# Seven block products instead of eight in three of eight units of the late gate and up pairs

## The chip, the cores and the metric

The kernel runs on one core of one Trainium2 chip. The metric is device time in microseconds. Three runs of the kernel before gave a median of 1877.37 us (1877.36 to 1877.59).

## The reference, cut to what matters

One layer of a decoder with 256 tokens of width 2048: a mixer (gated linear attention and sparse attention, merged), then a gated feed-forward block, then a norm. All is float32. The change touches the feed-forward block, whose weights are 2048 x 11264 (gate and up side by side) and 5632 x 2048:

```python
def swiglu(h, w_gate_up, w_down):
    g, u = jnp.split(h @ w_gate_up, 2, axis=-1)
    return (jax.nn.silu(g) * u) @ w_down
...
        h = rms_norm(x, norm2_gain[layer]) * (1.0 + sc2) + sh2
        x = x + g2 * swiglu(h, w_ffn_gate_up[layer], w_ffn_down[layer])
    return rms_norm(x, final_norm_gain)
```

## The kernel before, in words

**A block product.** TensorE takes a 128 x 128 block of activations as the stationary operand and streams 128 x 512 of weights past it. To keep float32 accuracy, both are split in two parts, a rounded one (float32r, "hi") and what is left (the rest, "lo"). One block product is three matmuls into one PSUM bank: hi by hi, hi by lo, lo by hi (L351 to L353 in `main`). The activations are split once (tiles `h`, `gA`, `gB`); the weights are split as they arrive: ScalarE casts (L311) and VectorE subtracts (L313), 1024 columns at a time.

**An item** (`Mm`) is four contraction blocks of 128 rows by 512 columns, 1 MB, loaded by one DMA from SP (L272) into one of three `raw` buffers. It has two token halves, so 4 x 2 x 3 = 24 matmuls. `hi` and `lo` have four buffers of 1024 columns each, two of which an item takes.

**The order** is written out: the list `items`, walked by `run`. After the matmuls of an item come (where it is the last of its group) the evacuation, the preparing of items ahead (`pres`, two ahead) and one step of each of the side threads (`qa`, `qb`, `qc`), as far as a credit of 3.6 us an item allows. Each engine works its own queue in the order in which this loop issues.

**The feed-forward block** has three parts of 4, 4 and 3 column blocks of 512 (`FF_PARTS`). In each part, each column block has a gate group and an up group (four items each, two of the four main PSUM banks each), then four down groups follow over the part's columns. The gate is evacuated by a Silu (L1240), the up by a product (L1244); the result is transposed on TensorE (L1057, eight transposes a block, in two steps of the thread `qb`, into the three auxiliary banks `pa`), cast (L1062) and its rest formed (L1063). The down groups read it; `need` waits for the transposes of the last block. A down group's evacuation adds to the residual (L1278, L1279).

**PSUM** has eight banks: four main (`pm`), three auxiliary (`pa`), one held (`ph`, used earlier in the attention).

**Row buffers.** `g2_start` (L1263) loads the gate's row and the final gain's row into the two `gr` buffers, on ScalarE's DMA queue. `acc` is one more buffer of 2048 columns.

Of the kernel before, what the change touches and what calls it, by code (L numbers as in the profile page):

```python
# [35 lines left out]
SLOT = 3.6  # L36
ORDER = "d0 a0 a1 d1 a2 a3 d2 y0 y1 d3 y2 y3"
FF_PARTS = ((0, 4), (4, 4), (8, 3))
NEG = -1.0e30
FILL = -3.0e38  # L40
TAKEN = -3.4e38
# [16 lines left out]
        self.ahead = AHEAD  # L58


class Grp:
    def __init__(self, act, evac, need=None, late=False, cost=0.6):
        self.act, self.evac, self.need, self.late, self.cost, self.ps = act, evac, need, late, cost, None
        self.mid = None


class Lr:
# [41 lines left out]
def tile_layer(tc, x, c, positions, norm1_gain, norm2_gain, w_ada, b_ada, w_in, gate_up, gate_bias,  # L109
# [3 lines left out]
    with (  # L113
# [140 lines left out]
        def load(it):  # L254
            if it.extra:
                raw = work("raw", EARLY_RAWS, [128, D])
            else:
                raw = stp.tile([128, D], F32, tag="raw", bufs=RAW_BUFS, name=name("raw"))
            if isinstance(it, Mm):
# [12 lines left out]
            sp.dma_start(it.raw, src)  # L272
# [15 lines left out]
        def pre_mm(it, rests_last=False):  # L288
# [28 lines left out]
            for rest in rests:  # L317
                yield
                rest()

        def pre(its):

            gens = [(pre_ada if isinstance(it, Ada) else pre_mm)(it) for it in its]
            while gens:
                for g in gens[:]:
                    if next(g, gens) is gens:
                        gens.remove(g)

        def main(it):
            if isinstance(it, Lr):  # L330
                ps = psum_main()
                for kt in range(KT):
                    pe.matmul(ps[0:32], it.both[:, kt].rearrange("p v n -> p (v n)"),
                              h1[:, kt].rearrange("p a t -> p (a t)"), start=kt == 0, stop=kt == KT - 1)
                it.evac(ps)
                return
            g = it.grp
            if it.first:
                g.ps = [psum_main() for _ in range(2)]
                g.deferred = []  # L340
            parts = [(hv[:, k], lv[:, k]) for hv, lv in it.hl for k in range(hv.shape[1])]

            def products(it, parts, k, t):
                kt = it.k0 + k
                if g.need:
                    g.need(kt, t)
                xh, xl = g.act(kt)
                hv, lv = parts[k]
                o = g.ps[t][:, 0:it.nc]
                a, b = xh[:, t * 128:(t + 1) * 128], xl[:, t * 128:(t + 1) * 128]  # L350
                pe.matmul(o, a, hv, start=it.first and k == 0, stop=False)  # L351
                pe.matmul(o, a, lv, start=False, stop=False)  # L352
                pe.matmul(o, b, hv, start=False, stop=it.last and k == it.nk - 1)  # L353

            for k in range(it.nk):
                for t in range(1 if it.defer or it.by_token else 2):
                    products(it, parts, k, t)
            if it.defer or it.by_token:
                g.deferred.append((it, parts))
            if it.by_token:  # L360
                for d, dparts in g.deferred:
                    for k in range(d.nk):
                        if g.mid and d is it and k == MID:
                            g.mid(g.ps)
                        products(d, dparts, k, 1)
            it.hl = None

        def run():
# [47 lines left out]
            for it in items:  # L416
# [10 lines left out]
                if late_evac:  # L427
                    late_evac()
                    late_evac = None
                early_evac = isinstance(it, Mm) and it.last and it.by_token  # L430
# [617 lines left out]
                qb.add(m_transposes(n))  # L1048
            return f

        def split_transposes(src, kt0, dst):

            for i in range(2):
                ps = psum_aux()
                for a in range(2):
                    for t in range(2):
                        pe.transpose(ps[:, a * S + t * 128:a * S + t * 128 + 128],  # L1057
                                     src[:, t, (i * 2 + a) * 128:(i * 2 + a + 1) * 128], ident)
                kt = kt0 + i * 2
                hi = dst[kt // 8][:, kt % 8:kt % 8 + 2, :].rearrange("p a t -> p (a t)")  # L1060
                lo = dst[2 + kt // 8][:, kt % 8:kt % 8 + 2, :].rearrange("p a t -> p (a t)")
                act.copy(hi, ps)  # L1062
                dve.tensor_sub(lo, ps, hi.bitcast(F32))  # L1063
                yield 0.7
# [180 lines left out]
                    qb.add(ff_transposes(a, kt0))  # L1245
            return f

        def ff_transposes(a, kt0):
# [4 lines left out]
            for cost in split_transposes(a, kt0, late["act"]):  # L1253
                late["ready"] += 2
                yield cost

# [5 lines left out]

        def g2_start():  # L1263
            late["g2"] = bcast_row("gr", b_ada[5 * D:6 * D])
            late["fg"] = g8("gr")
            act.dma_start(late["fg"], final_gain.unsqueeze(0).to_broadcast([128, D]))

        def g2_rows():
            for n in range(4):
# [46 lines left out]
        for p, (g0, ng) in enumerate(FF_PARTS):  # L1316
            ex = spread(0) if p == 0 else None
            at_first = len(items)
            for n in range(ng):
                if p == 0 and n == 1:  # L1320
                    items.append(Call(g2_start))
                for which in range(2):
                    add_group(w_ffn_up, which * DFF + (g0 + n) * 512, 512,
                              Grp(act_h2, up_evac(which, n, n * 4), need_h2), extra=ex if n else None)
# [57 lines left out]
```

## Time and profile before

| what | value |
|---|---|
| median of 3 runs | 1877.37 us |
| the profiled execution | 1878.03 us |
| its span (first to last instruction) | 1875.9 us |
| TensorE busy | 1832.3 us, 98% |
| VectorE busy | 1285.0 us, 69% |
| ScalarE busy | 853.4 us, 45% |
| GpSimd (POOL) busy | 115.4 us, 6% |
| granted TensorE clock, mean | 0.994 |

Busy shares are means over the whole span. In the span's second half the table of 40 slices has VectorE at 4 to 7 tenths and the DMA engines at 5 to 8, and TensorE at 9 in every slice but the last, which is 8. PE is TensorE, PEld its weight loads, DVE VectorE, ACT ScalarE; a name with q is the DMA issue of that engine. A matmul's shown duration includes its way through the array, so consecutive ones overlap; the pitch is read from the starts.

### The profile page before, as it was taken

How to read it: one execution, taken by the hardware profiler on the slowest of the kernel's cores; microseconds unless marked ns; L12 is line 12 of the kernel's file. 1: busy time of each engine (PE TensorE's matmuls, PEld its weight loads, DVE VectorE, ACT ScalarE, POOL GpSimd, SP SyncE). 2: the span in 40 equal slices, each digit the busy share in tenths (PEclk: the TensorE clock that was granted, in tenths of full speed). 3: DMA queues.
4: the chain of work that ended last, by engine and by line, in shares of the span. 5: the costliest groups of instructions: out<-in, count | busy, mean ns of one | idle time of the engine just before them, and what ended most of it. 6: DMA issues, size and time to landing. Idle time of an engine off the chain costs nothing.

```text
span 1875.9 us, 23110 instructions
## 1 busy us (share of the span) xinstructions
PE 1832.3 (98%) x9132; PEld 1507.8 (80%) x9132; DVE 1285.0 (69%) x1441; ACT 853.4 (45%) x1114; POOL 115.4 (6%) x141
## 2 busy tenths in 40 slices
PE   3999999999999999999999999999999999999998
PEld 2888888877788888888888787888788888888886
DVE  6899865798765678787778566777555445554455
ACT  4554443655645444444444445444334444334443
POOL 0000000533220100200000000000000000000002
PEclk8999999999999999999999999999999999999999
DMA  9998743534445787888888754889555555655553
GB/s 363 386 358 315 281 165 106 202 136 141 153 158 173 270 307 282 295 301 296 298 326 314 254 202 151 335 309 325 177 186 199 186 196 180 199 186 198 180 180 133
DMA packets 198077, 440.89 MB, mean 235 GB/s; under 512 B 7832, under 2 KB 14128, under 8 KB 188880
## 3 DMA queue, kind: packets, MB, share of 16 engines
q1 hardware_dynamic: 196544, 433.69, 65.7%
q10 hardware_dynamic: 1424, 5.72, 0.8%
q8 instruction: 71, 1.16, 0.2%
q14 instruction: 38, 0.31, 0.0%
HBM read 437.29 MB, written 2.10 MB: 234 GB/s over the span
## 4 chain that ended last, share of the span: by engine, by line
PE 92%; DVE 4%; issue 2%; ACT 1%; DMA 1%; POOL 0%; SPq 0%; POOLq 0%; ACTq 0%; DVEq 0%
PE pm L351 29%; PE pm L353 29%; PE pm L352 29%; DVE acc L285 1%; DVE lo L313 1%; PE pa L1057 1%; PE pa L980 0%; DVE acc L679 0%; ACT hi L311 0%; DMA raw<-in_w_ada_dram 0%; PE pa L951 0%; PE pa L1003 0%; PE pa L906 0%; PE pa L487 0%; PE ph L686 0%
## 5 line engine op out<-in xcount | busy, mean ns | idle before, releaser
L313 DVE TENSOR_TENSOR lo<-raw,hi 128x1024 fp32r<-128x1024 f32 (+1 forms) x630 | 764.3, 1223 | 526.6 <-ACT hi L311 526.1
L311 ACT CAST hi<-raw 128x1024 fp32r<-128x1024 f32 (+1 forms) x630 | 651.7, 1043 | 892.0 <-PE pm L353 687.2
L351 PE MATMUL pm<-hi,h 128*128 128x512 f32 (+1 forms) x1784 | 699.0, 392 | 2.2 <-ACT h L470 1.9
L353 PE MATMUL pm<-hi,h 128*128 128x512 f32 (+1 forms) x1784 | 690.4, 387 | 0.0
L352 PE MATMUL pm<-lo,h 128*128 128x512 f32 (+1 forms) x1784 | 689.4, 386 | 0.2 <-DVE lo L313 0.2
L351 PEld LDWEIGHTS pm<-hi,h 128*128 128x128 f32 x1784 | 335.8, 188 | 70.3 <-ACT h L470 2.3
L353 PEld LDWEIGHTS pm<-hi,h 128*128 128x128 f32 x1784 | 335.3, 188 | 68.7 <-DVE h L477 0.2
L352 PEld LDWEIGHTS pm<-lo,h 128*128 128x128 f32 x1784 | 335.9, 188 | 66.4 <-DVE lo L313 0.7
L351 PE MATMUL pm<-hi,gA 128*128 128x512 f32 x608 | 242.0, 398 | 0.0
L353 PE MATMUL pm<-hi,gB 128*128 128x512 f32 x608 | 237.0, 390 | 0.0
L352 PE MATMUL pm<-lo,gA 128*128 128x512 f32 x608 | 236.8, 389 | 0.2 <-DVE lo L313 0.2
L285 DVE SCALAR_TENSOR_TENSOR acc<-raw,sc,acc 128x2048 f32<-128x2048 f32 (+2 forms) x122 | 218.1, 1788 | 3.1 <-DMA raw<-in_w_ada_dram 2.2
L352 PEld LDWEIGHTS pm<-lo,gA 128*128 128x128 f32 x608 | 114.3, 188 | 25.4 <-issue 1.7
L351 PEld LDWEIGHTS pm<-hi,gA 128*128 128x128 f32 x608 | 114.2, 188 | 24.7 <-issue 1.9
L353 PEld LDWEIGHTS pm<-hi,gB 128*128 128x128 f32 x608 | 114.1, 188 | 23.9
L1283 POOL TENSOR_TENSOR gC<-gC,gr 128x512 f32<-128x512 f32 x3 | 4.9, 1638 | 718.0 <-ACT pm L1281 718.0
L670 POOL TENSOR_TENSOR acc<-gC 128x512 f32<-128x512 f32 x32 | 39.2, 1236 | 38.5 <-DVE acc L679 38.1
L679 DVE TENSOR_TENSOR acc<-gB,acc 128x256 f32<-128x256 f32 x64 | 31.2, 546 | 6.9 <-ACT acc L674 6.8
L988 ACT ACTIVATE S<-S,mx 128x128 f32<-128x128 f32 (+1 forms) x32 | 14.3, 448 | 32.3 <-DVE mx L986 32.3
L784 POOL TENSOR_TENSOR rp<-tm,sin 128x128 f32<-128x128 f32 x9 | 8.3, 922 | 306.6 <-ACT tm L932 183.8
L674 ACT ACTIVATE acc<-acc 128x256 f32<-128x256 f32 x64 | 22.3, 415 | 6.8 <-POOL acc L670 6.7
L351 PE MATMUL pm<-hi,gr 128*128 128x512 f32 x64 | 24.9, 389 | 0.0
(271 smaller groups left out, 1040.2 us busy)
## 6 DMA issues: line engine op xcount, KB each, us to landing
raw<-in_w_in_dram SPq DMA_DIRECT2D x129, 1024.0 KB, 4.8
raw<-in_w_ffn_gate_up_dram SPq DMA_DIRECT2D x88, 1024.0 KB, 4.9
raw<-in_w_ada_dram SPq DMA_DIRECT2D x64, 1024.0 KB, 4.8
raw<-in_w_ffn_down_dram SPq DMA_DIRECT2D x44, 1024.0 KB, 5.1
raw<-in_w_ada_dram SPq DMA_DIRECT2D x64, 512.0 KB, 8.5
raw<-in_w_branch_gla_dram SPq DMA_DIRECT2D x16, 1024.0 KB, 5.1
raw<-in_w_branch_dsa_dram SPq DMA_DIRECT2D x16, 1024.0 KB, 5.3
raw<-in_w_merge_out_dram SPq DMA_DIRECT2D x16, 1024.0 KB, 5.1
```

Of the source, the lines that this page charges most:

```text
L285: dve.scalar_tensor_tensor(a[:, g], it.raw[:, j, g], s, a[:, g], ALU.mult, ALU.add)
L311: act.copy(hv, src)
L313: rests.append(lambda lv=lv, src=src, hv=hv: dve.tensor_sub(lv, src, hv.bitcast(F32)))
L351: pe.matmul(o, a, hv, start=it.first and k == 0, stop=False)
L352: pe.matmul(o, a, lv, start=False, stop=False)
L353: pe.matmul(o, b, hv, start=False, stop=it.last and k == it.nk - 1)
L670: pool.tensor_tensor(d, v, v[:, :, s - 1:s].to_broadcast([128, n, 2 * s]), ALU.subtract)
L674: act.activation(d, d, AF.Exp, scale=(1.0 if u else -1.0) / 16)
L679: dve.tensor_tensor(w, src, d, ALU.mult)
L784: pool.tensor_tensor(u, a, si, ALU.mult)
L988: act.activation(nst[:, a:b], nst[:, a:b], AF.Exp, bias=mx[:, t:t + 1], accum_out=sm[:, t:t + 1])
L1057: pe.transpose(ps[:, a * S + t * 128:a * S + t * 128 + 128], src[:, t, (i * 2 + a) * 128:(i * 2 + a + 1) * 128], ident)
```

## The change

The gate and up groups of parts 1 and 2 (seven pairs) are worked together. A `Unit` is two contraction blocks by 512 gate columns and the same 512 up columns: a 2 x 2 grid of weight blocks, against a 2 x 2 grid of activation blocks (two token halves, two contraction blocks). Eight units make a pair. The result is four blocks of 128 x 512.

In units 2, 4 and 6 (`THRIFTY`) the four results are had from seven block products of sums of blocks instead of eight. The sums of activation blocks are formed once, split and kept (`more_forms`, tile `x`), as steps of `qb` beside the down groups of part 0. The sums of weight blocks are formed by VectorE as the weights arrive, then cast and given rests (`pre_unit`). The other five units form eight products, into the same seven banks' scheme. Seven banks collect partial results (four main, three auxiliary); seven additions at the pair's end (`unit_evacs`, `early`) make the four blocks.

In the five full units the rest of two of the four weight blocks is not made by VectorE: ScalarE writes the negative, rounded, and a DMA issued from POOL adds the weights to it. These rests have two buffers (`added`, in the second `gr` buffer), and are begun ahead of the unit's casts.

The transposes of parts 1 and 2 use the one held bank, one step later. The down group 3 of parts 0 and 1 is evacuated ahead of the preparing. A unit is loaded by two DMAs of half the size. The final gain's row is loaded at the last part's down groups. At the third down group of part 0 the tile pool `work` is closed and `units` opened.

```diff
+THRIFTY = (2, 4, 6)
...
+            if isinstance(it, Unit):
+                it.raw = raw.rearrange("p (k s n) -> p k s n", k=2, s=2)
+                rows = it.w[it.k0 * 128:it.k0 * 128 + 256, :].rearrange("(k p) n -> p k n", p=128)
+                for i in range(2):
+                    sp.dma_start(it.raw[:, :, i], rows[:, :, it.c0 + i * it.step:it.c0 + i * it.step + 512])
+                return
...
+        def pre_unit(it):
+
+            b = it.raw.rearrange("p k s n -> p (k s) n")
+            part = lambda h, l, i: (h[:, i], l[:, i])
+            if not it.thrifty:
+                thrift["n"] = 1 - thrift.get("n", 0)
+                added = thrift["added"][:, thrift["n"]]
+                act.mul(added, b[:, 2:4], -1.0)
+                pool.dma_start(added, b[:, 2:4], accum_op=ALU.add)
+                hv, lv = split_tile("hi"), split_tile("lo")
+                act.copy(hv, b[:, 0:2])
+                dve.tensor_sub(lv, b[:, 0:2], hv.bitcast(F32))
+                it.b11, it.b12 = part(hv, lv, 0), part(hv, lv, 1)
+                yield
+                hv = split_tile("hi")
+                act.copy(hv, b[:, 2:4])
+                it.b21, it.b22 = part(hv, added, 0), part(hv, added, 1)
+                yield
+                return
+            t, th, tl = thrift["t"], thrift["hi"], thrift["lo"]
+            hv, lv = split_tile("hi"), split_tile("lo")
+            act.copy(hv, b[:, 2:4])
+            dve.tensor_tensor(t, b[:, 0:4:3], b[:, 1:2].to_broadcast([128, 2, 512]), ALU.add)
+            dve.tensor_sub(lv, b[:, 2:4], hv.bitcast(F32))
+            it.b21, it.b22 = part(hv, lv, 0), part(hv, lv, 1)
+            yield
+            dve.tensor_tensor(b[:, 3], b[:, 3], t[:, 0], ALU.add)
+            dve.tensor_tensor(b[:, 1], b[:, 3], b[:, 2], ALU.add)
+            hv, lv = split_tile("hi"), split_tile("lo")
+            act.copy(hv, b[:, 0:2])
+            dve.tensor_sub(lv, b[:, 0:2], hv.bitcast(F32))
+            it.b11, it.t4 = part(hv, lv, 0), part(hv, lv, 1)
+            yield
+            act.copy(th[:, 0:2], t)
+            act.copy(th[:, 2], b[:, 3])
+            dve.tensor_sub(tl[:, 0:2], t, th[:, 0:2].bitcast(F32))
+            dve.tensor_sub(tl[:, 2], b[:, 3], th[:, 2].bitcast(F32))
+            it.t1, it.t3, it.t2 = (part(th, tl, i) for i in range(3))
+            yield
...
+        def main_unit(it):
+            g = it.grp
+            if it.first:
+                g.ps = {m: psum_main() for m in (2, 4, 5, 3)} | {m: psum_aux() for m in (1, 6, 7)}
...
+            if it.thrifty:
+                s3, s1, s2, s4 = (ext(i) for i in range(4))
+                todo = ((3, s4, it.b22), (2, a12, it.b21), (1, a11, it.b11), (4, a22, it.t4),
+                        (5, s1, it.t1), (7, s3, it.t3), (6, s2, it.t2))
+            else:
+                todo = ((2, a11, it.b11), (4, a21, it.b11), (5, a21, it.b12), (3, ext(0), it.b12),
+                        (2, a12, it.b21), (4, a22, it.b21), (5, a22, it.b22), (3, ext(1), it.b22))
...
+            for m, (xh, xl), (hv, lv) in todo:
...
+                pe.matmul(o, xh, hv, start=m not in g.begun, stop=False)
+                pe.matmul(o, xh, lv, start=False, stop=False)
+                pe.matmul(o, xl, hv, start=False, stop=stop)
...
+                if isinstance(it, Unit) and it.last:
+                    it.grp.early(it.grp.ps)
                 pres(ahead=getattr(it, "ahead", AHEAD))
...
+        def ff_transposes(a, kt0, bank=psum_aux):
...
             yield
+            if bank is psum_held:
+                yield
+            for cost in split_transposes(a, kt0, late["act"], bank):
...
+        def more_forms():
...
+            for j in range(KT // 2):
...
+                dve.tensor_tensor(a.rearrange("p (k t) -> p k t", k=2), hv, lv, ALU.add)
...
+                if j in THRIFTY:
+                    dve.tensor_sub(d3, a11, a21)
+                    dve.tensor_sub(d1, a21, a22)
+                    dve.tensor_sub(d2, d1, a11)
+                    dve.tensor_tensor(d4, a12, d2, ALU.add)
+                else:
...
+                    dve.tensor_sub(f[:, 0:256].rearrange("p (k t) -> p k t", k=2), av[:, :, 0:128], av[:, :, 128:256])
...
+                act.copy(hi, fv)
+                dve.tensor_sub(lo, fv, hi.bitcast(F32))
...
+            def early(ps):
+                a = t4("fA")
+                u = t4("fC")
+                act.copy(a[:, 0], ps[1])
+                dve.tensor_tensor(u[:, 0], a[:, 0], ps[6], ALU.add)
+                dve.tensor_tensor(u[:, 1], u[:, 0], ps[7], ALU.add)
+                dve.tensor_tensor(a[:, 0], a[:, 0], ps[2], ALU.add)
+                dve.tensor_tensor(a[:, 1], u[:, 1], ps[4], ALU.add)
+                dve.tensor_tensor(u[:, 1], ps[5], u[:, 1], ALU.subtract)
+                dve.tensor_tensor(u[:, 0], ps[5], u[:, 0], ALU.subtract)
+                dve.tensor_tensor(u[:, 0], u[:, 0], ps[3], ALU.add)
+                act.activation(a, a, AF.Silu)
...
+            def rest(ps):
...
+                dve.tensor_tensor(a, a, u, ALU.mult)
+                qb.add(ff_transposes(a, n * 4, psum_held))
...
+                if p:
+                    eager, rest = unit_evacs(n)
+                    grp = Grp(None, rest, need_forms, cost=6.0)
...
+                if p == 0 and n == 2:
+                    items.append(Call(thrift_start))
+                if p == 2 and n == 0:
+                    items.append(Call(final_gain_row))
...
+                items[-1].grp.soon = p < 2 and n == 3
```

## Rows read from the trace of the kernel before

**Rows 1.** The page's busy table: engine, us, share, instructions.
```profile
PE 1832.3 (98%) x9132; PEld 1507.8 (80%) x9132; DVE 1285.0 (69%) x1441; ACT 853.4 (45%) x1114; POOL 115.4 (6%) x141
```

**Rows 2.** The chain of waits that ended last: shares by engine and line.
```profile
PE 92%; DVE 4%; issue 2%; ACT 1%; DMA 1%; POOL 0%; SPq 0%; POOLq 0%; ACTq 0%; DVEq 0%
PE pm L351 29%; PE pm L353 29%; PE pm L352 29%; DVE acc L285 1%; DVE lo L313 1%; PE pa L1057 1%; PE pa L980 0%; DVE acc L679 0%; ACT hi L311 0%; DMA raw<-in_w_ada_dram 0%; PE pa L951 0%; PE pa L1003 0%; PE pa L906 0%; PE pa L487 0%; PE ph L686 0%
```

**Rows 3.** Windows: pairs of part 1, its down groups, pairs of part 2.
```profile
core 0: us, PE busy (x) PEld busy (x) DVE busy (x) ACT busy (x) POOL busy (x), PEclk, DMA share, GB/s
1403.00:1581.00 178.00, 178.00 (x798) 147.36 (x797) 88.26 (x81) 75.05 (x79) 0.00 (x0) 1.00 0.56 191
1581.00:1669.00 88.00, 88.00 (x394) 72.85 (x393) 49.02 (x49) 34.72 (x34) 0.00 (x0) 1.00 0.57 191
1669.00:1802.00 133.00, 133.00 (x596) 110.10 (x595) 66.55 (x61) 55.48 (x58) 0.00 (x0) 1.00 0.56 190
```

**Rows 4.** Waits, 1380 to 1870 us: who <- whom, us in total, times, longest.
```profile
ACT hi L311 <- PE pm L353: 268.0, 165, 1.7
DVE lo L313 <- ACT hi L311: 227.6, 163, 1.7
...
PE pm L352 <- DVE lo L313: 0.2, 1, 0.2
```

**Rows 5.** Timeline, TensorE: start us, us; two matmuls twelve apart.
```profile
1506.46 0.39 PE L351 MATMUL pm<-hi,h 128*128 128x512 f32 x1
...
1509.18 0.39 PE L351 MATMUL pm<-hi,h 128*128 128x512 f32 x1
```

**Rows 6.** Groups by line and form, 1480 to 1860 us: count, busy us, mean ns.
```profile
L313 DVE TENSOR_TENSOR lo<-raw,hi 128x1024 fp32r<-128x1024 f32 x137 | 168.9, 1236 | 178.9 <-ACT hi L311 178.9
L311 ACT CAST hi<-raw 128x1024 fp32r<-128x1024 f32 x137 | 144.1, 1054 | 211.2 <-PE pm L353 210.0 <-ACT hi L311 1.2
...
L1278 DVE TENSOR_TENSOR fC<-gr,pm 128x512 f32<-128x512 f32 x14 | 9.5, 679 | 0.0
L1063 DVE TENSOR_TENSOR gB<-pa,gA 128x512 fp32r<-128x512 f32 x12 | 8.2, 683 | 0.0
L1062 ACT CAST gA<-pa 128x512 fp32r<-128x512 f32 x12 | 6.9, 578 | 0.0
...
L1279 DVE TENSOR_TENSOR gC<-gC,fC 128x512 f32<-128x512 f32 x7 | 4.8, 691 | 0.2
...
L1240 ACT ACTIVATE fA<-pm 128x512 f32<-128x512 f32 x6 | 3.2, 589 | 0.0
```

**Rows 7.** DMA issues, 1380 to 1870 us: count, KB each, median us to landing.
```profile
raw<-in_w_ffn_gate_up_dram SPq DMA_DIRECT2D x56, 1024.0 KB, 4.8
...
out_dram<-gC SPq DMA_DIRECT2D x2, 512.0 KB, 2.7
```

**Rows 8.** DMA queues and issues, 0 to 50 us: packets, MB, share of 16 engines.
```profile
q1 hardware_dynamic: 8531, 17.86, 96.3%
...
raw<-in_w_ada_dram SPq DMA_DIRECT2D x24, 512.0 KB, 10.8
```

**Rows 9.** Timeline: the last block's first transposes and what follows them.
```profile
1805.49 0.60 PE L1057 MATMUL pa<-cc,fA 128*128 128x128 f32 x4
...
1805.69 1.05 ACT L311 CAST hi<-raw 128x1024 fp32r<-128x1024 f32 x1 [1.67 <-PE pm L353]
...
1805.85 0.47 PE L351 MATMUL pm<-hi,gA 128*128 128x512 f32 x1
...
1806.65 0.58 ACT L1062 CAST gA<-pa 128x512 fp32r<-128x512 f32 x1
1806.78 1.22 DVE L313 TENSOR_TENSOR lo<-raw,hi 128x1024 fp32r<-128x1024 f32 x1 [1.50 <-ACT hi L311]
1807.92 0.68 DVE L1063 TENSOR_TENSOR gB<-pa,gA 128x512 fp32r<-128x512 f32 x1
```

**Rows 10.** Groups by line and form, 0 to 1480 us.
```profile
L477 DVE TENSOR_TENSOR h<-mod,h 128x256 fp32r<-128x256 f32 x16 | 6.7, 420 | 4.2 <-ACT mod L472 4.0
```

More of the change, by code (lines that the diff above doesn't have):

```diff
@@ L58, in __init__ @@
         self.ahead = AHEAD
+class Unit(Mm):
+    def __init__(self, w, k0, c0, step, grp, first, last, thrifty, x0):
+        super().__init__(w, k0, 2, c0, 512, grp, first, last)
+        self.step, self.thrifty, self.x0 = step, thrifty, x0
 class Grp:
@@ new lines, in tile_layer @@
+        thrift = {}
+        def main_unit(it):
+            g = it.grp
+            if it.first:
+                g.ps = {m: psum_main() for m in (2, 4, 5, 3)} | {m: psum_aux() for m in (1, 6, 7)}
+                g.begun = set()
+            if g.need:
+                g.need(it)
+            h, x = late["h2"], thrift["x"]
+            a11, a12, a21, a22 = ((h[:, it.k0 + k, 0, t * 128:t * 128 + 128], h[:, it.k0 + k, 1, t * 128:t * 128 + 128])
+                                  for t in range(2) for k in range(2))
+            ext = lambda i: (x[:, it.x0 + i, 0], x[:, it.x0 + i, 1])
+            if it.thrifty:
[5 more added lines that the diff above has]
+                        (2, a12, it.b21), (4, a22, it.b21), (5, a22, it.b22), (3, ext(1), it.b22))
+            left = [m for m, _, _ in todo]
+            for m, (xh, xl), (hv, lv) in todo:
+                left.remove(m)
+                stop = m not in left and (it.last or it.k0 == g.last_thrifty and m in (1, 6, 7))
+                o = g.ps[m]
+                pe.matmul(o, xh, hv, start=m not in g.begun, stop=False)
+                pe.matmul(o, xh, lv, start=False, stop=False)
+                pe.matmul(o, xl, hv, start=False, stop=stop)
+                g.begun.add(m)
@@ L321, in pre @@
         def pre(its):
-            gens = [(pre_ada if isinstance(it, Ada) else pre_mm)(it) for it in its]
+            gens = [(pre_ada if isinstance(it, Ada) else pre_unit if isinstance(it, Unit) else pre_mm)(it) for it in its]
             while gens:
@@ L336, in main @@
                 return
+            if isinstance(it, Unit):
+                return main_unit(it)
             g = it.grp
@@ L1246, in up_evac @@
             return f
-        def ff_transposes(a, kt0):
+        def ff_transposes(a, kt0, bank=psum_aux):
             if kt0 == 0:
@@ L1264, in g2_start, with final_gain_row, thrift_start @@
             late["g2"] = bcast_row("gr", b_ada[5 * D:6 * D])
-            late["fg"] = g8("gr")
+        def final_gain_row():
+            late["fg"] = bp.tile([128, D], F32, tag="acc", bufs=1, name=name("acc"))
             act.dma_start(late["fg"], final_gain.unsqueeze(0).to_broadcast([128, D]))
+        X0 = [sum(4 if j in THRIFTY else 2 for j in range(k)) for k in range(KT // 2 + 1)]
+        def thrift_start():
+            nonlocal wp
+            qb.drain()
+            late_pools.close()
+            wp = late_pools.enter_context(tc.tile_pool(name="units", bufs=1))
+            thrift["x"] = work("x", 1, [128, X0[-1], 2, 128], F32R)
+            thrift["t"] = work("t", 1, [128, 2, 512])
+            thrift["hi"] = bp.tile([128, D], F32R, tag="acc", bufs=1, name=name("acc")).rearrange("p (s n) -> p s n", n=512)
+            thrift["lo"] = work("lo", 1, [128, 3, 512], F32R)
+            thrift["added"] = g8("gr", F32R).rearrange("p (i s n) -> p i s n", i=2, s=2)
+            qb.add(more_forms())
@@ new lines, in need_forms, with unit_evacs @@
+        def need_forms(it):
+            if "formed" not in state:
+                qb.drain(lambda: state.get("forms") == KT // 2 - 1)
+                state["formed"] = True
+        def unit_evacs(n):
+            def early(ps):
[10 more added lines that the diff above has]
+                act.activation(a, a, AF.Silu)
+                ff["a"], ff["u"] = a, u
+            def rest(ps):
+                a, u = ff["a"], ff["u"]
+                dve.tensor_tensor(a, a, u, ALU.mult)
+                qb.add(ff_transposes(a, n * 4, psum_held))
+            return early, rest
@@ L1321, in tile_layer @@
                     items.append(Call(g2_start))
+                if p:
+                    eager, rest = unit_evacs(n)
+                    grp = Grp(None, rest, need_forms, cost=6.0)
+                    grp.early, grp.last_thrifty = eager, 2 * max(THRIFTY)
+                    for j in range(KT // 2):
+                        items.append(Unit(w_ffn_up, 2 * j, (g0 + n) * 512, DFF, grp, j == 0, j == KT // 2 - 1,
+                                          j in THRIFTY, X0[j]))
+                    continue
                 for which in range(2):
```

25 lines of the change are left out of this document (19 added, 6 removed).

## The prediction, made before the changed kernel ran

> **What bounds the kernel now.** I read the page's busy table first: TensorE is busy for 98% of the span [rows 1]. The chain of waits says the same from the other end: 92% of the chain that ended last is TensorE, in three lines (L351, L352, L353) of equal weight, the three matmuls of one block product [rows 2]. By stretches (the late gate and up pairs, the down products between them, the last pairs), TensorE has no gap, VectorE is busy for half the time and the DMA engines for 0.56 of it, all at full granted clock [rows 3]. The waits of this part say who paces whom: ScalarE's cast waits for TensorE to give a buffer back (L353 ends it) and VectorE for that cast; TensorE itself waited once, for 0.2 us [rows 4]. So time here is the number of matmuls times their pitch. The pitch: the same line starts at 1506.46 and, twelve matmuls on, at 1509.18, so 2.72 / 12 = 0.2267 us; a unit of 24 takes 5.44 us [rows 5].
>
> **What the change removes.** Three of the eight units of a pair form 7 products instead of 8: three matmuls less each, 9 a pair, 63 over seven pairs. 63 x 0.2267 = 14.3 us, all on the path. A pair is then 183 matmuls = 41.5 us, with its eight transposes (two sets at 0.36: the next matmul starts at 1805.85 where it would have come near 1805.49 [rows 9]) about 42.2.
>
> **What it adds, term by term.**
>
> *Casts and sums.* A short unit (2, 4, 6) asks of VectorE four operations on 1024 columns and three on 512: 4 x 1.24 + 3 x 0.69 = 7.0 us; a full unit one of 1024, 1.24. The end of a pair asks for seven sums from PSUM at 0.68, a product of 1024 and two rests at 0.68: 7.4 us [rows 6]. A pair: 3 x 7.0 + 5 x 1.24 + 7.4 = 34.6 of 42.2 us. In each short unit VectorE also stands still while ScalarE casts the two sums, 1.05 us: 37.8. ScalarE: five full units at 3 x 1.05, three short ones at 3 x 1.05 + 0.6, the end of the pair (three casts of 0.58, a Silu of two 512s at 0.59) 2.9: 30 us. Both fit, VectorE with 4.4 us to spare, and units are prepared two ahead. I cost this at nothing; the cover is that spare time, and each microsecond over it costs 7.
>
> *All banks at once.* A pair now holds four main banks, and the next needs them back. The order of the sums gives them in the order of need. From the end of unit 7, bank 2 is complete at -2.0 and read by -1.2, bank 4 by -0.5, bank 5 by +0.9 (needed at +1.4, the third product), bank 3 by +1.5 (needed at +2.0), at 0.68 a sum. Half a microsecond spare; nothing, if VectorE comes in time. The down groups give theirs back in the same way (evacuation first in parts 0 and 1), with 0.5 to 1 us spare.
>
> *Rests by DMA.* Five units of a pair have half their rests made by an accumulating DMA from POOL: 35 of 512 KB. No row shows one. From below: the 512 KB store at the end lands in 2.7 us. The 1024 KB load of this very stretch, as many bytes as an accumulation has to read (source and destination), takes 4.8 [rows 7]. From above: the 512 KB loads of the first 50 us, with the engines 96% taken, land in 10.8 [rows 8]. I take 6: the 4.8, and about one more for sharing the engines with a load under way. How long may it take? Tightest is unit 1 of a pair: the two buffers alternate over five units, so unit 1 has that of the last pair's unit 7 and is freed at that unit's end (time 0). ScalarE first finishes the Silu (about 0.7), then writes the negative (1.05): the DMA starts at 1.7. Its rest is first read in the fifth product of unit 1: 5.44 + 13 x 0.2267 = 8.4. Room: 6.7 us, in five of seven pairs (the first pair of a part follows down groups, and its buffers are long free). Unit 5: its negative follows unit 4's last casts, which can start at the end of unit 2, so it is written 1.65 + 1.05 = 2.7 after that; its rest is read 5.44 + 4.76 + 2.95 = 13.15 after: 10.4, less some 1.5 for VectorE's sums ahead of those casts, about 9. The others have more. At 6 it costs nothing. At 2.7 also nothing; at 10.8 it costs 5 x 4.1 + 7 x 1.8 = 33.
>
> *The weights behind them.* A raw buffer is now kept until the accumulation has read it, and SP's next load waits in its queue for that. With three buffers, the load of unit i + 3 still has some 10 us before it is wanted, and lands in 4.8 [rows 7]. The engines: 1 MB is 0.56 x 5.44 = 3.05 us of all sixteen [rows 3]; an accumulation 1.5 to 3.05 (bytes counted once or twice); a pair 8 x 3.05 + 5 x (1.5 to 3.05) = 32 to 39.7 of 42.2 us. Full but not over. The load in two halves has the same rows; nothing.
>
> *More forms of the activations*, eight steps beside the down groups of part 0: with 0.42 (256 columns) as an upper bound for each small operation [rows 10], 3 x 3.1 + 5 x 1.5 = 17 us of VectorE over eight units of 5.44, in a stage where it is busy 49 of 88 us [rows 3]: 94%. Rests there are ready some 5.9 us early (a cast starts when a buffer comes free and cast and rest take 2.3, three half units, 8.2 us, before use). Nothing.
>
> *Transposes of the last pair.* Here I see a loss. With one held bank instead of three, the steps come one unit later. In parts of four groups nothing needs them by then, but part 2 has three, and the third down unit reads them at once. Its first set is issued right in front of its use, the second in its middle. Before, from the next matmul at 1805.85, the cast was done at 1807.23 and the rest at 1808.60 [rows 9], while TensorE ran on. Now it waits: 1.4 for the cast, then, two matmuls later, 0.9 for the rest: 2.3 a set, 4.6 for two. Without the casts ahead of them on ScalarE and VectorE it would be 1.1 a set, 2.2. I take 4, nearer to the row.
>
> *The final gain's row* is loaded later, on ScalarE's queue, into a buffer whose last reader ended a unit before, and read 20 us later; nothing.
>
> **Sum.** Against the profiled execution's own 1878.03 us (span 1875.9, 2.1 around it): 1878.0 - 14.3 + 4.0 = 1867.7. That execution stands 0.7 above the median of the runs, so against the median 1867.0: 10.4 us, 0.55%, faster.
>
> **Rivals.**
> *Rests come late (slower).* Each microsecond that an accumulation takes beyond 6.7 stops TensorE in unit 1 of five pairs, and beyond 9 in unit 5 of all. For it: no row shows POOL's DMA, its two reads and one write share engines that I count up to 94% full, and 512 KB once took 10.8. Against: that was at 96%. Time at 10.8: 1867 + 33 = 1900. From about 8 (6.5 lost) it is no gain that a measurement can tell (0.2%, 3.75 us, about what can be told here), from 9.2 slower.
> *VectorE holds off POOL (slower).* If POOL cannot write its transfer's orders while VectorE reads two operands from SBUF, an issue waits for a gap: a short unit has 1.24 + 1.24 + 0.69 + 0.69 = 3.9 us without one. An accumulation of 6 becomes up to 9.9: 5 x 3.2 + 7 x 0.9 = 22, 1889. The rows neither show nor exclude it: POOL issues no DMA in them. The Trainium skill (SBUF — State Buffer, "SBUF: two separate sides") tells of such a trap: descriptors of a DMA issued from GpSimd cannot be written while VectorE holds the shared ports; but it limits this to VectorE's two-port modes, and for operations with two SBUF inputs to a GpSimd operation that reads SBUF. The operations here have two inputs. No run here shows which holds.
> *VectorE becomes the bound (about the same).* If the pair's chain on VectorE, 37.8 by my count, comes to 43.8, through waits between ScalarE and VectorE that I have not seen, each pair loses 1.5: 1867 + 10.5 = 1877.5. For: the sums of a pair's end keep VectorE from running ahead from the fifth product of unit 7 on. Against: 4.4 us of room.
> *The matmuls saved are not time (about the same).* If the pitch of the rest rose by 0.011 us with waits at each new operand, 1281 matmuls would eat 14 us: 1877 + 4 = 1881 with the transposes, 1877 without. Against: today's pitch is the same whichever tiles are read, 0.2267, and the weight loads are beside it.
>
> **How the numbers follow.** Forecast 0.58; rests late 0.18; POOL held off 0.06; VectorE the bound 0.11; pitch 0.07. Faster by over 0.2%: the forecast and a mild case of VectorE as the bound, 0.60. Within 0.2%: the rest of that case, most of the pitch's, the mild cases of late rests, 0.18. Slower: 0.22. Predicted 1867. Low end: 1877.4 - 14.3 = 1863 with no loss at all. High end: 1884, which takes in accumulations up to about 9.4 us (5 x 2.7 + 7 x 0.4 = 16 lost, 1883) and one more for the transposes at 4.6; beyond lie one to two chances in ten. The forecast's own range is 1863 to 1873.
>
> **What would show it.** TensorE with 63 matmuls less; POOL's 35 transfers landing in 5 to 7 us after issue; in the waits, TensorE hardly waiting for a DMA in the fifth product of unit 1, and twice for some 2 us for a cast or rest in the third down unit of part 2; VectorE's total up by some 11 us a pair and 17 for the forms, near 1375; the DMA share of the pairs between 0.75 and 0.94. Wrong, if TensorE waits in every pair for the accumulation (first rival: landing over 8; second: landing normal once issued, the issue late) or for a rest from VectorE (third).

## The result: slower by 0.9%, because the rests added by DMA come late

| | median us | ratio to before, 95% interval |
|---|---|---|
| before | 1877.36 | |
| the change | 1894.91 (1892.13 to 1896.39, 5 runs) | 1.0093 [1.0078, 1.0108] |

The profiled execution took 1895.57 us, its span is 1893.6. TensorE issues the 63 matmuls less that were forecast, so 14.3 us were saved and some 31.8 lost again. The page's busy table and the chain of waits, after:

```profile
PE 1830.2 (97%) x9069; PEld 1497.1 (79%) x9069; DVE 1377.3 (73%) x1586; ACT 916.8 (48%) x1199; POOL 146.4 (8%) x176
...
PE 76%; DVE 8%; DMA 8%; ACT 4%; issue 3%; POOL 0%; SPq 0%; ACTq 0%; POOLq 0%; DVEq 0%
PE pm L447 23%; PE pm L449 23%; PE pm L448 23%; DMA gr<-raw 4%; DMA raw<-in_w_ffn_gate_up_dram 3%; DVE lo L334 2%; DVE acc L306 1%; PE pm L411 1%; PE pm L412 1%; PE pm L410 1%; ACT hi L332 1%; DVE lo L368 1%; ACT gr L352 1%; PE pa L1078 0%;
```

VectorE's total is what was forecast (1375). But the chain, 92% TensorE before [rows 2], is now 76%, and a transfer stands in it that was not there: `gr<-raw`, the accumulation. The waits of 1380 to 1890 us (who <- whom, us in total, times, longest) and the accumulation's row among the DMA issues say how often:

```profile
PEld pm L411 <- DMA gr<-raw: 26.2, 23, 2.6
...
PE pm L411 <- DMA gr<-raw: 16.7, 18, 2.2
...
PEld pm L410 <- DVE fC L1447: 2.6, 2, 1.8
...
PEld pm L447 <- ACT gA L1160: 2.3, 2, 1.4
...
PE pm L447 <- ACT gA L1160: 1.9, 2, 1.2
...
PE pm L410 <- DVE fC L1447: 1.7, 2, 1.4
```

```profile
raw<-in_w_ffn_gate_up_dram SPq DMA_DIRECT2D x112, 512.0 KB, 4.8
...
gr<-raw POOLq DMA_DIRECT2D x35, 512.0 KB, 8.1
```

L411 is the second matmul of a block product, which reads the rest: 23 times TensorE waited for one that had not landed; before it waited once, 0.2 us, in the whole stretch [rows 4]. The median landing is 8.1 us, where 6 was taken. Added up from TensorE's starts, the stops are 20.1 us for the rests (20 of them: some 4.8 us in unit 1, 1.7 in unit 3, 8.1 in unit 5, 5.6 in unit 7), 2.1 for banks (L410 after down groups) and 2.8 for the last transposes. What follows a stop can cost as well. TensorE's timeline after one of 2.17 us (start, us, idle before <- releaser), and the windows around it:

```profile
1460.10 0.50 PE L411 MATMUL pm<-gr,h 128*128 128x512 f32 x1 [2.17 <-DMA gr<-raw]
1460.43 0.39 PE L412 MATMUL pm<-hi,h 128*128 128x512 f32 x1
1460.66 0.42 PE L410 MATMUL pm<-hi,h 128*128 128x512 f32 x1
1460.89 0.62 PE L411 MATMUL pm<-gr,h 128*128 128x512 f32 x1
1461.31 0.63 PE L412 MATMUL pm<-hi,h 128*128 128x512 f32 x1
1461.74 0.63 PE L410 MATMUL pm<-hi,h 128*128 128x512 f32 x1
```

```profile
1452.00:1456.00 4.00, 4.00 (x20) 3.30 (x19) 4.00 (x4) 1.88 (x2) 0.08 (x1) 1.00 0.96 290
1461.00:1463.00 2.00, 2.00 (x6) 1.54 (x5) 1.60 (x3) 1.50 (x2) 0.86 (x1) 0.50 0.77 207
...
1466.00:1470.00 4.00, 4.00 (x22) 3.30 (x21) 3.80 (x5) 1.15 (x2) 0.00 (x0) 1.00 0.99 296
```

The pitch goes from 0.23 to 0.43 us soon after TensorE starts again, and is back 3.4 us later: the granted clock (third number from the right) is 0.50 there, the lower of the two levels, 1.2 GHz. The busy table counts this loss as busy; starts and clock show it. It is not behind every stop. Of the stops for rests only this one, the longest, was followed by it; one of 1.53 us, for instance, was not:

```profile
1528.89 0.50 PE L411 MATMUL pm<-gr,h 128*128 128x512 f32 x1 [1.53 <-DMA gr<-raw]
```

```profile
1529.00:1533.00 4.00, 4.00 (x18) 3.31 (x19) 2.04 (x3) 3.05 (x3) 0.86 (x1) 1.00 0.69 222
```

Between 1380 and 1880 us the lower clock comes once more, for as long, behind the stop for a bank at 1404.70 (1.37 us); in f1 below, the stop at that place is 1.56 us and the clock stays at 1.00. What decides it isn't shown. The two stretches cost 3.3 us. Besides, the first matmul behind a stop takes 0.33 us to the next start (1460.10 to 1460.43) and not 0.23: 2.5 us in all. 20.1 + 2.1 + 2.8 + 3.3 + 2.5 = 30.8 of the 17.5 (lost) + 14.3 (saved) = 31.8; the last microsecond is spread thinly over the other starts.

### The profile page after: what moved, and what is told of

It is laid out like the page before. It is cut to its first block, busy times and chain, and to the rows that moved or that the text cites. A ratio compares the mean times of both kernels' runs of the same rounds, so it can differ in the third digit from the quotient of the medians.

```text
span 1893.6 us, 23556 instructions
## 1 busy us (share of the span) xinstructions
PE 1830.2 (97%) x9069; PEld 1497.1 (79%) x9069; DVE 1377.3 (73%) x1586; ACT 916.8 (48%) x1199; POOL 146.4 (8%) x176
## 4 chain that ended last, share of the span: by engine, by line
PE 76%; DVE 8%; DMA 8%; ACT 4%; issue 3%; POOL 0%; SPq 0%; ACTq 0%; POOLq 0%; DVEq 0%
PE pm L447 23%; PE pm L449 23%; PE pm L448 23%; DMA gr<-raw 4%; DMA raw<-in_w_ffn_gate_up_dram 3%; DVE lo L334 2%; DVE acc L306 1%; PE pm L411 1%; PE pm L412 1%; PE pm L410 1%; ACT hi L332 1%; DVE lo L368 1%; ACT gr L352 1%; PE pa L1078 0%; DVE acc L777 0%
## 5 line engine op out<-in xcount | busy, mean ns | idle before, releaser
L334 DVE TENSOR_TENSOR lo<-raw,hi 128x1024 fp32r<-128x1024 f32 (+2 forms) x518 | 626.9, 1224 | 356.1 <-ACT hi L332 355.8
L332 ACT CAST hi<-raw 128x1024 fp32r<-128x1024 f32 (+2 forms) x518 | 531.5, 1040 | 683.0 <-PE pm L449 471.3
L447 PE MATMUL pm<-hi,h 128*128 128x512 f32 (+1 forms) x1336 | 523.4, 392 | 2.2 <-ACT h L568 1.9
L449 PE MATMUL pm<-hi,h 128*128 128x512 f32 (+1 forms) x1336 | 515.8, 386 | 0.0
L448 PE MATMUL pm<-lo,h 128*128 128x512 f32 (+1 forms) x1336 | 515.2, 386 | 0.2 <-DVE lo L334 0.2
L447 PEld LDWEIGHTS pm<-hi,h 128*128 128x128 f32 x1336 | 251.7, 188 | 53.3 <-ACT h L568 2.3
L449 PEld LDWEIGHTS pm<-hi,h 128*128 128x128 f32 x1336 | 251.3, 188 | 50.9 <-DVE h L575 0.2
L448 PEld LDWEIGHTS pm<-lo,h 128*128 128x128 f32 x1336 | 251.7, 188 | 49.1 <-DVE lo L334 0.7
L449 PEld LDWEIGHTS pm<-hi,gB 128*128 128x128 f32 x608 | 114.1, 188 | 25.2 <-DVE gB L1161 1.5
L410 PE MATMUL pm<-hi,h 128*128 128x512 f32 x252 | 99.5, 395 | 1.4 <-DVE fC L1447 1.4
L412 PE MATMUL pm<-hi,h 128*128 128x512 f32 x252 | 99.3, 394 | 0.0
L356 DVE TENSOR_TENSOR lo<-raw,hi 128x1024 fp32r<-128x1024 f32 x35 | 42.9, 1225 | 37.7 <-ACT hi L355 37.7
L411 PE MATMUL pm<-gr,h 128*128 128x512 f32 x105 | 44.4, 423 | 16.9 <-DMA gr<-raw 16.7
L410 PEld LDWEIGHTS pm<-hi,h 128*128 128x128 f32 x252 | 47.9, 190 | 12.0 <-DVE fC L1447 1.8
L411 PE MATMUL pm<-lo,h 128*128 128x512 f32 x147 | 57.2, 389 | 0.0
```

What stands on the lines that cost most here:

```text
L332: act.copy(hv, src)
L334: rests.append(lambda lv=lv, src=src, hv=hv: dve.tensor_sub(lv, src, hv.bitcast(F32)))
L356: dve.tensor_sub(lv, b[:, 0:2], hv.bitcast(F32))
L410: pe.matmul(o, xh, hv, start=m not in g.begun, stop=False)
L411: pe.matmul(o, xh, lv, start=False, stop=False)
L412: pe.matmul(o, xl, hv, start=False, stop=stop)
```

## Experiments

Theory A: accumulations take some 8 us, rests come late, TensorE stops. Theory B: VectorE is the bound. Theory C: VectorE's two-input operations hold off POOL's transfers. The first four runs take one part away each.

**e1.** The accumulation is left out; half the rests of five units are then the rounded negative alone.
```diff
-                pool.dma_start(added, b[:, 2:4], accum_op=ALU.add)
```


> The accumulating DMA is left out (the rests of five units keep the negative alone, so those numbers are not the layer's); all else stays, VectorE's and ScalarE's work too. Theory A (TensorE waits for accumulations that land after 8.1 us instead of 6, and loads wait for the buffers that they keep): the 26 us of waits and slow clock in the pairs go, the 2.8 us at the last transposes stay: 1866 to 1869. Theory B (VectorE's chain of a short unit is the bound, and the accumulation only happens to be late): over 1885, with TensorE waiting for rests from VectorE.

1869.69 us, ratio 0.996 [0.9946, 0.9975]. The accumulations cost 25.2 us: the 20.1 of stops, and what lies behind these. TensorE's waits in the stretch are then those for banks and transposes, and one of 0.6.

**e2.** VectorE forms all rests, as in the short units.
```diff
-                act.mul(added, b[:, 2:4], -1.0)
-                pool.dma_start(added, b[:, 2:4], accum_op=ALU.add)
+                dve.tensor_sub(lv, b[:, 2:4], hv.bitcast(F32))
```


> No accumulation; VectorE forms the five rests of 1024 columns a pair too. By theory A the only bound left is VectorE's count: 34.6 + 5 x 1.24 + 3 x 1.05 = 44.0 us a pair against 42.2 of TensorE, so 1.8 lost in each of seven pairs on top of 1867: about 1880 (1874 to 1886). By theory B, where VectorE is the bound already at 46 us a pair, it adds 6.2 a pair: over 1930.

1870.35, ratio 0.9964 [0.9951, 0.9977]: faster than before, with nothing left out. Both theories had it slower than that (A about 1880, 1874 at the least; B over 1930). Its windows, two stretches of pairs (columns as in [rows 3]):

```profile
1400.00:1560.00 160.00, 157.60 (x704) 129.08 (x703) 143.62 (x159) 82.12 (x95) 0.00 (x0) 1.00 0.57 192
1670.00:1760.00 90.00, 90.00 (x404) 74.54 (x403) 79.64 (x85) 49.66 (x57) 0.00 (x0) 1.00 0.56 190
```

VectorE is busy for 143.62 of 160 us, 0.90, and TensorE for all of 1670 to 1760. B falls: there was room for the work that the DMA was to take over.

**e3.** One short unit (2) instead of three, the same five accumulations; VectorE is then busy for 0.51 to 0.53 of the pairs.
```diff
-THRIFTY = (2, 4, 6)
+THRIFTY = (2,)
+BY_DMA = (0, 1, 3, 5, 7)
```


> One short unit (2) instead of three; the same five units have their accumulation, units 4 and 6 their rests from VectorE. VectorE falls to some 26 of 43.6 us a pair and has no long stretches from unit 3 on; the loads stay as dense. Theory A (the transfer shares the engines with the loads): landing stays at 7.5 to 8.5 us; time, with more room for it, 1875 to 1882. Theory C (VectorE's two-operand operations hold off POOL's transfer): landing falls to 5 to 6 us, time about 1875.

1892.97, ratio 1.0089 [1.0072, 1.0106], landing 7.6. With VectorE idle for half of the time the accumulations land hardly sooner (in units 3, 5 and 7 medians of 7.5, 8.9 and 9.4 us, as against 7.5, 8.8 and 9.4 in the change): against C. A's time was missed as well, by 11 us. The stops for rests are 10.3 us in place of 20.1, but two more full units in each pair bring back 42 of the 63 matmuls, 9.5 us.

**e4.** The same transfer without the adding; what stands where the rests should be are then the weights themselves.
```diff
-                pool.dma_start(added, b[:, 2:4], accum_op=ALU.add)
+                pool.dma_start(added, b[:, 2:4])
```


> The DMA from POOL copies the weights and adds nothing (so the rests are wrong): same bytes written, the destination is not read. If the second read makes it long, it lands in some 6 us and the time falls to 1870 to 1876. If it waits behind the loads (theory A), the wait to its first packet (3.5 us in the middle) stays and only the transfer shortens: lands in 7 to 7.5, time 1880 to 1888.

1868.96, ratio 0.9959 [0.9944, 0.9973]; landing 4.8, no wait for a rest. VectorE's work is that of the change here, which tells against C again. I read this as: reading the destination makes the transfer long. The last four runs show that this was half of it.

**f1, f2, f3.** On e2, one edit more each: the transposes of the last pair one unit sooner; the forms (`thrift_start`) one down group sooner; and in short units VectorE forms a rest while ScalarE casts the sums.
```diff
-            if bank is psum_held:
+            if bank is psum_held and not last:
                 yield
```
```diff
-                if p == 0 and n == 2:
+                if p == 0 and n == 1:
                     items.append(Call(thrift_start))
```
```diff
+            act.copy(th[:, 0:2], t)
             dve.tensor_tensor(b[:, 3], b[:, 3], t[:, 0], ALU.add)
             dve.tensor_tensor(b[:, 1], b[:, 3], b[:, 2], ALU.add)
+            dve.tensor_sub(tl[:, 0:2], t, th[:, 0:2].bitcast(F32))
...
-            act.copy(th[:, 0:2], t)
...
-            dve.tensor_sub(tl[:, 0:2], t, th[:, 0:2].bitcast(F32))
```


> As e2_vector_rests (no accumulation, 1870.35), and the last pair's transposes begin one unit earlier. The three waits in the third down unit of part 2 (1.2, 0.8 and 0.7 us) go: 1867.6 (1866 to 1869). If the loss there were only moved (the held bank is taken again at once), it stays at 1870.

> As f1_early_transposes, and the forms of the activations begin one down group earlier, so that none is queued on VectorE in front of the last evacuation of part 0. If that order makes the waits of 1.7, 0.5 and 0.7 us at the first units (and the slow clock after them, some 2 us), they go: 1862 to 1865. If the evacuation itself is too slow for the next pair's banks, the wait stays: 1867 to 1868.

> As f2_forms_early, and in a short unit VectorE forms two rests while ScalarE casts the two sums, instead of standing still for 1.05 us. VectorE has been shown not to be the bound in the pairs (no wait for it there in e2): no change against f2, within 0.5 us. If it was close to being the bound: 1 to 2 us less.

1867.12, 0.9948 [0.9935, 0.996]; 1864.04, 0.9929 [0.9915, 0.9942]; 1862.99, 0.9926 [0.9914, 0.9938]. The transposes cost 3.2 us and the forms 3.1; the third step is 1.05, within the spread of the runs. Why the forms cost: VectorE's timeline after down group 3 of part 0, in the change:

```profile
1400.81 0.69 DVE L1391 TENSOR_TENSOR t<-h 128x512 f32<-128x512 f32 x1
...
1402.38 0.29 DVE L1398 TENSOR_TENSOR t<-t 128x128 f32<-128x128 f32 x1
1403.36 0.69 DVE L1406 TENSOR_TENSOR x<-t,x 128x512 fp32r<-128x512 f32 x1 [0.69 <-ACT x L1405]
1403.97 0.68 DVE L1447 TENSOR_TENSOR fC<-gr,pm 128x512 f32<-128x512 f32 x1
```

A step of the forms, with a wait for ScalarE in it, is queued ahead of the evacuation (L1447) that gives the bank back; TensorE's next first product starts at 1404.70, 1.37 us late.

**f4.** Accumulations in units 0 and 3 alone, VectorE the other three. If full DMA engines make them long, two should land soon.
```diff
+BY_DMA = (0, 3)
...
+                by_dma = it.k0 // 2 in BY_DMA
+                if by_dma:
```


> The change with two accumulations a pair (units 0 and 3) instead of five; VectorE forms the other three rests. Theory A (the engines are so full that a transfer waits): the engines' share falls from 0.86 to about 0.7, the landing to 6 to 7 us, the waits for rests nearly vanish: 1869 to 1873, near e2_vector_rests (1870.35). If an accumulation takes its 8 us however many there are: landing 8, and still some 3 us lost a pair where unit 3 waits: 1876 to 1885.

1879.59, ratio 1.0014 [1.0005, 1.0022]; landing 7.5 although the DMA share is down to 0.72. So neither how many there are nor how full the engines are on average makes them long.

**g1, g2.** Is it the load that SP issues within 0.3 us of an accumulation? A small copy on SP's queue was to hold it back, with two accumulations (g1) and five (g2).
```diff
+                if by_dma:
+                    sp.dma_start(state["later"], hv[:, 1, 0:8].bitcast(F32))
```


> As f4_two_adds (units 0 and 3, landing 7.5 us, 1879.6), but SP's next load is held back until the unit's second cast is done, some 2 us after POOL's issue, by a 4 KB copy in front of it on SP's queue. Theory A, made narrower (a load issued 0.3 us after the accumulation reaches the DMA engines ahead of it, since the accumulation's own start takes longer, and goes first): landing falls to 5 to 5.5 us, TensorE's waits for rests go, 1870 to 1873. Rival D (the accumulation itself needs its 7.5 us): landing stays, 1878 to 1882.

> The change itself (five accumulations a pair) with the loads held back behind them in the same way. Narrow theory A: landing from 8.1 to about 6; the loads come 2 us later than they could, so some of the gain is lost again: 1872 to 1884. Rival D: landing 8, and the later loads make it slower still: over 1895.

1879.59, 1.0012 [1.0002, 1.0021]; 1893.67, 1.0097 [1.008, 1.0114]; landing 7.4 and 7.7. Inconclusive: in g1's trace the copy comes to SP 1.3 us after the load that it was to hold back.

**g3.** On e2: POOL itself subtracts, in place of a transfer.
```diff
-                dve.tensor_sub(lv, b[:, 2:4], hv.bitcast(F32))
+                pool.tensor_sub(lv, b[:, 2:4], hv.bitcast(F32))
```


> As e2_vector_rests (1870.35), but the second rest of each full unit is a subtraction on POOL instead of VectorE: 35 of 1024 columns, at 1.2 to 1.6 us for 512 columns some 2.5 to 3.3 each. If VectorE and POOL work side by side: VectorE's operations keep 1.22 us and the time stays at 1868 to 1872. Theory C's mechanism (operations with two operands from SBUF on VectorE and POOL shut each other out): VectorE's 34.6 and POOL's 13 to 16 us a pair add up to more than 42.2: 1900 to 1935.

1889.18, ratio 1.0066 [1.0051, 1.0081]. Its groups by line and form, 1420 to 1580 us (count, busy us, mean ns):

```profile
L357 POOL TENSOR_TENSOR lo<-raw,hi 128x1024 fp32r<-128x1024 f32 x18 | 53.3, 2966 | 118.7 <-ACT hi L356 118.7
...
L364 DVE TENSOR_TENSOR t<-raw 128x1024 f32<-128x1024 f32 x11 | 29.2, 2657 | 0.0
...
L365 DVE TENSOR_TENSOR lo<-raw,hi 128x1024 fp32r<-128x1024 f32 x11 | 13.3, 1213 | 0.0
```

VectorE's 1024-column operation takes 2.66 us where POOL runs beside it (L364) and 1.21 where it doesn't (L365). The Trainium skill (SBUF — State Buffer, "SBUF: two separate sides") says that a VectorE operation with two SBUF inputs and a GpSimd operation that reads SBUF exclude each other; these rows agree. They bear on POOL's arithmetic, and say nothing for C: POOL's accumulating issues took 0.85 to 0.87 us all through the pairs of the change and in h1, all but the first (1.10).

**h1.** Open was whether the load ahead or the adding makes an accumulation long. Two accumulations as in f4, but unit 3's is begun ahead of the casts of unit 2's sums, so ahead of the load that those casts' end lets go.
```diff
+            if it.k0 // 2 in (2,):
+                begin_added(it.next)
             act.copy(th[:, 0:2], t)
             act.copy(th[:, 2], b[:, 3])
```


> The change with accumulations in units 0 and 3 of a pair alone; ScalarE writes unit 3's negative, and POOL issues its accumulation, ahead of the casts of unit 2's two sums, some 1.6 us sooner, and so ahead of the load that unit 2's release lets go. Theory 'load ahead' (the accumulation is long because a 1 MB load, issued 0.3 us after it, starts before it): unit 3's accumulations land in 5 to 5.5 us, those of unit 0 as before, and no product of unit 3 waits; 1869 to 1873. Theory 'own length' (reading the destination makes it long, loads or not): they land in 7 to 8 us as before; begun 1.6 sooner they still end waits of 0.8, so 1870 to 1874. The landing time tells them apart, not the total.

1870.44, ratio 0.9966 [0.9953, 0.9979]. Unit 3's accumulation lands in 4.8 to 4.9 us in each of the seven pairs, those of unit 0 in 6.7 to 7.6 (the very first in 5.0). The issues of f4 and of h1 in the same pair; SP's next load issue is 0.29 us behind POOL in the first and 2.52 behind in the second (f4, then h1):

```profile
1463.85 0.86 POOL L356 DMA_DIRECT2D gr<-raw  x1 [19.51 <-ACT gr L355]
...
1464.14 0.88 SPq L279 DMA_DIRECT2D raw<-in_w_ffn_gate_up_dram  x2
```

```profile
1458.53 0.86 POOL L354 DMA_DIRECT2D gr<-raw  x1 [17.13 <-PE pm L424]
...
1461.05 3.38 SPq L280 DMA_DIRECT2D raw<-in_w_ffn_gate_up_dram  x4
```

So "load ahead" holds: 7.5 against 4.9 for the same adding, although in f4 the load is issued a little behind POOL. VectorE is busy for 136.56 of 160 us here, more than in the change (34.56 of 47), and the landing is shorter: against C once more.

**h2.** Begun sooner still, in ScalarE's idle 5 us ahead of unit 2's second cast.
```diff
             act.copy(hv, b[:, 2:4])
+            if it.k0 // 2 in (2,):
+                begin_added(it.next)
```


> As the last, but unit 3's negative is written before unit 2's second cast, while ScalarE waits some 5 us for VectorE's sums: about 6 us sooner than in the change. Theory 'late' (the only loss is TensorE's wait for the rests and the slow clock after it): no wait for a rest, granted clock 1.00 in the pairs, 1869 to 1873 whatever the landing. Theory 'disturbance' (an accumulation costs time by what it does to loads and engines, waited for or not): 1877 to 1880 as with the same two accumulations at their old place.

1870.57, ratio 0.9962 [0.9947, 0.9977]; landing 6.6 (median of both units) and no wait for a rest. An accumulation that nobody waits for costs nothing that shows (e2, without any: 1870.35). Unit 3's takes 5.6 to 7.3 us where a load was issued 1.1 to 1.9 ahead of it, and 4.5 to 4.7 where none was within 3 us.

**h3.** All five accumulations of the change: those of units 5 and 7 begun as in h2, that of 3 as in h1, that of 1 where it was.

> All five accumulations of the change; those of units 5 and 7 begun some 6 us sooner (before the second cast of units 4 and 6), that of unit 3 some 1.6 sooner (before the casts of unit 2's sums; its buffer is not free before); that of unit 1 where it was, since its buffer comes free no sooner. Theory 'late': only unit 1 still waits, 1.5 to 2.3 in five pairs, with a slow clock after it: 11 + 3 left of 20 + 6, so 1880 to 1886. Theory 'disturbance': 1890 to 1895.

1879.38 (1874.14 to 1885.02, 10 runs), ratio 1.0013 [1.0001, 1.0025]; a touch under the range of "late". The profiled execution is its fastest (1874.14), so its waits (five for rests, 4.1 us on the weight loads) are less than the median's. The landing is 4.9 in the median, and even unit 1's, which was not moved, lands in 5.1 to 5.6 in six of seven pairs (9.3 in the first), since the load beside it now comes behind it. The change, then h3, at unit 1:

```profile
1450.44 0.88 SPq L278 DMA_DIRECT2D raw<-in_w_ffn_gate_up_dram  x2
...
1451.23 0.85 POOL L353 DMA_DIRECT2D gr<-raw  x1 [7.02 <-ACT gr L352]
```

```profile
1449.76 0.85 POOL L354 DMA_DIRECT2D gr<-raw  x1 [7.13 <-ACT gr L353]
...
1450.94 1.67 SPq L280 DMA_DIRECT2D raw<-in_w_ffn_gate_up_dram  x2
```

The first landed in 8.8 us, the second in 5.5. Over all 28 accumulations of units 1, 3, 5 and 7 of the change: 27 have a load issued between 1.9 us ahead of POOL's and 0.3 behind, and land in 6.1 to 10.9 us; the one whose load came 2.4 behind lands in 5.2. In h3, with the load 0.9 to 2.5 behind or none near, 4.5 to 5.6; with one 1.6 ahead and another within 0.4 (unit 0 of five pairs, which has time), 9.0 to 9.4.

**h4.** Accumulations in units 0, 3, 5, 7, the last three begun as in h2; unit 1 by VectorE; with the edits of f1 and f2.
```diff
+BY_DMA = (0, 3, 5, 7)
...
+            if it.k0 // 2 in (2, 4, 6):
+                begin_added(it.next)
```


> Accumulations in units 0, 3, 5 and 7, the last three begun some 6 us sooner, unit 1's rest formed by VectorE; and the two edits tried before: the transposes of the last pair one unit sooner, the forms begun one down group sooner. Theory 'late': no wait for a rest at a landing of 7 to 8, 1864 to 1867, as with no accumulation at all (1864.0). Theory 'disturbance': over 1872.

1862.45 (1862.24 to 1864.22), ratio 0.9923 [0.9908, 0.9938]; a little under the 1864 to 1867 of "late". TensorE has no gap in the pairs, with the DMA share still at 0.84:

```profile
1400.00:1560.00 160.00, 160.00 (x719) 132.44 (x718) 127.25 (x139) 97.86 (x111) 12.87 (x15) 1.00 0.84 249
1670.00:1780.00 110.00, 110.00 (x495) 91.04 (x494) 87.21 (x95) 68.79 (x79) 8.60 (x10) 1.00 0.84 246
```

Here theory C falls for good. At 1534.40 POOL issues unit 3's accumulation, and VectorE is busy for 1.37 of the next 1.40 us with operations that read two operands from SBUF; the accumulation lands in 4.9 us. At 1668.84 of the change VectorE is idle for all of the 1.40 us behind POOL's issue, a load follows 0.03 us behind it, and the accumulation lands in 7.3 (h4, then the change; columns as in [rows 3]):

```profile
1534.40:1535.80 1.40, 1.40 (x8) 1.16 (x7) 1.37 (x2) 0.00 (x0) 0.86 (x1) 1.00 1.04 401
```

```profile
1668.84:1670.24 1.40, 1.40 (x8) 1.17 (x7) 0.00 (x0) 0.99 (x1) 0.86 (x1) 1.00 0.35 32
```

The kernel of h4 beats both kernels, and the change by 32.5 us. f3, without any accumulation, is as fast within the intervals (1862.99).

## Why the prediction was wrong

*What the change removes*: right. 63 matmuls less, and f3 and h4 end 14.2 and 14.8 us under the before that ran beside them (1877.23, 1877.29), against 14.3 from the count.

*Rests by DMA* is the step that failed, by two of its numbers. The landing: 6 us was taken from a row of loads that shared the engines with no transfer of another queue [rows 7], plus one for sharing. The accumulation takes 4.9 when it is begun ahead of the load, which is under that, but in this order of work its negative is finished just as the casts release the raw buffer that the next load waits for, and half of the load or more mostly moves first: medians of 7.3, 7.5, 8.8 and 9.4 in units 1, 3, 5 and 7. The step *The weights behind them* counted engine time for this pair of transfers, and not which of the two moves first. The room: 6.7 in unit 1 was right (6.5 by the trace); but unit 5, given 9, has 6.9 to 7.9, and "the others have more" was wrong: unit 3 has 6.8 to 7.1, unit 7 8.4 to 9.3. So unit 1, "tightest" in the prediction, makes less than a quarter of the stops, and unit 5 the most. The formula at the median landing of 8.1 would give 5 x 1.4 = 7 us. Measured are 25.2 (e1): 20.1 of stops, since units 3, 5 and 7 stop as well, at the landing of their own place, and some 5 behind the stops (2.2 at the first matmuls, 1.6 at the lower clock, 1.3 not traced), which the prediction did not price at all.

How a load delays the accumulation the trace's DMA records show. In unit 3 of the change (issue at 1509.05, load issued 0.29 us behind) half of the load moves first, from 2.0 to 4.5 us after the issue, then the accumulation, from 3.7 to 7.2, then the load's other half, from 5.3 to 8.5. In h1 (issue at 1500.98) the accumulation moves from 1.4 to 4.6 and the load begins behind, at 4.3. So the accumulation itself takes as long, 3.1 to 3.5 us, and starts later; in units 1, 3, 5 and 7 of the change it starts 1.8 to 5.3 us after the issue and takes 3.0 to 6.0. The Trainium skill (DMA: Bandwidth & Descriptors, "Queues, rings and completion order") has each DMA engine take turns between queues, a whole packet of descriptors at a time. This order agrees with such turns if half a load counts as one packet, which the records do not show. Why the load gets the first turn although it is issued 0.29 us behind stays open; the plain copy of e4 at that place begins 1.1 us after its issue.

*More forms* was priced "Nothing", with the rests' reserve as its cover. The rests were not what suffered: the evacuation, in the same queue of VectorE, came late (2.1 us of stops in the change, and some 1.6 at the lower clock behind them; 3.1 by f2, on f1, which stops there for 2.3 and, for a rest, 0.6 and keeps its clock). *All banks at once* had that place as safe "if VectorE comes in time".

*Transposes of the last pair*: right in mechanism, 4 forecast, 2.8 in waits and 3.2 by f1.

*Casts and sums*: right; VectorE's 1377 us against 1375, and even where VectorE is busy for 0.88 of the time (e2), it leaves TensorE without a gap (1670 to 1760 us). *The final gain*, and the pitch (0.227 at full clock): right.

Of the rivals, *rests come late* happened, at 18 in 100; its price was too low by units 3, 5 and 7 and by what follows a stop, so that the change is slower at a median landing of 8.1, where 9.2 was given as the point. *VectorE holds off POOL* and *VectorE becomes the bound* are refuted by h4 and by e2.

## What to carry to other kernels

A transfer's price is not its row in a quiet queue: ask which other transfer is issued within two microseconds of it, and which instruction lets both go; in h1, moving one issue ahead of two casts (1879.59 in f4, 1870.44 in h1) was worth as much as giving all this work to another engine (1870.35 in e2). Work with a deadline should be begun where its engine idles, not where its consumer is prepared. And price a stop of TensorE at a little more than its length: here some 5 us on 20 for the rests, part of it in a stretch at the lower clock behind the longest.

## What was not expected of the hardware

A stop of 2.17 us was followed by 3.4 us at a pitch of 0.43 instead of 0.23 us (granted clock 0.50); stops of 1.53 and 1.61 were not. An accumulation of 512 KB within SBUF lands in 4.5 to 5.6 us with no load issued just ahead of it (h3), a plain copy from the same queue in 4.8 under the loads of the change. A POOL subtraction of 128 x 1024 takes 2.97 us, against 1.22 on VectorE, and lengthens VectorE's beside it from 1.21 to 2.66.
